# Second norm's weight on ScalarE in the stored rows, and the last four down-projection units two by two

## Chip, cores and metric

The kernel runs on one core of one Trainium2 chip. The metric is the device time of one execution in microseconds; before the change it is 1226.35 us, the median of three runs (1225.46 to 1226.62). Lower is better.

## The reference

One layer of a hybrid encoder for 1024 prompt tokens and 64 sample tokens that share the weights (1088 columns in all; the model width is 1024).

```
hn   = rmsnorm(h, pre_mix_g);   proj = hn @ w_in            # first norm
mix  = concat(SSD heads(proj), pooling groups(proj)) @ w_out
h    = h + rmsnorm(mix, post_mix_g)                          # h1
hn   = rmsnorm(h, pre_ffn_g)                                 # second norm: x * rstd(x) * weight
f    = (silu(hn @ w_gate) * (hn @ w_up)) @ w_down            # FFN
h    = h + rmsnorm(f, post_ffn_g)                            # h2
gate = sigmoid(h @ w_ple_gate)
y    = h + rmsnorm((p @ w_ple_proj) * gate, ple_norm_g)
```

Here rmsnorm(x, g) is x / sqrt(mean(x*x) + eps) * g over the model width. All of it is in float32.

## The kernel before, in words

Activations lie transposed: model width on the 128 partitions (8 blocks), tokens on the free axis, in four chunks of 272 columns. A float32 product is made of float32r halves (high part by a ScalarE cast, low part by a VectorE subtraction in the helper `sub`, L416), so each block takes three matmuls of 272 columns.

After the mixer, `out_tile` makes the w_out product of a chunk, ScalarE moves it out of PSUM with the weight of the post-mix norm (L1518), and `post_mix` goes on by pairs of blocks (four pairs, tiles of 128x544): VectorE multiplies by the norm's rstd (L1422), the residual x is added (L1431 by GpSimd, or by VectorE, as the string `XM` says for each pair: G or D), the sum h1 is stored to DRAM for later, and the class `SumSq` squares it (ScalarE, L617) and sums the squares (VectorE, L624, then L635). `rstd_job` turns the sum into rstd: small matmuls (L527), nine tiny VectorE instructions (L532 to L561), four transposes that leave rstd spread over the partitions in a PSUM bank (L565). Then `norm` multiplies each of the eight blocks by weight and rstd in one VectorE instruction (L1457).

The FFN multiplies 2x2 block matrices with seven products instead of eight (Strassen's scheme). For each pair of chunks p, `hforms(p)` builds seven combinations of the normed h (`B11`, `B21`, `T1` to `T4`, `B22`): VectorE differences (L1489), ScalarE casts (L1477), low parts (L416, tile h_T or h_B). A unit of weights has seven combinations too, and `product(q, m, ...)` (L1642) is product m of pass q: A11*B11 is 1, A12*B21 is 2, S4*B22 is 3, A22*T4 is 4, S1*T1 is 5, S2*T2 is 6, S3*T3 is 7. Three PSUM areas serve a pass: Z takes products 1, 6, 7 and 4 one on top of the other, and between them a copy or an addition must have read Z; W takes product 2, X takes 5 and then 3. `ffn()` writes out the order on TensorE: product 1 of a pass, products 4 and 3 of the pass before, then 2, 6, 5, 7 of the pass, and `until(...)` holds a product back until the reader of Z (flags s1, u2, u3) or X (x1) has been issued. Gate and up units come first (`passes`), then the down-projection (`passes2`), whose results `accum` adds into the tiles F on VectorE (L1905, first time by a ScalarE copy, L1902).

The last two down-projection units, d1_9 and d2_9, have two blocks only and are cut by chunk pair: four short passes, d1_9 and d2_9 for the first two chunks (p=0), then both for the last two (p=1). A product there is six matmuls, and the next units follow at once. When all of F of a chunk is final (`f_ready`), its squares are summed (L617, L624, L635), rstd is made, and `post_ffn` multiplies (L2089), adds h1 (L2095 GpSimd, L2098 VectorE) and splits h2 into high (L2103) and low parts (L416, tile h). The gate product of the last stage (`run_k` L509 by blocks as they are ready, `run` L492) needs h2 of chunk 0 right after the last FFN product; its weights w_pg are split on ScalarE (L463) and VectorE (L416) meanwhile.

The order of every engine's instructions is fixed beforehand by a planner (`Layout`): each step is a generator that yields requests such as `("A", 0.48, at)`, engine, planned cost and what to wait for; A is ScalarE, D VectorE, E VectorE with both operands in SBUF, G GpSimd (the planner lets no E and G overlap), S the DMA queue on SyncE, P TensorE. The planner picks the earliest start, then the lower priority number. A DMA counts as landed (`at`) 2 us plus columns divided by a rate (680 a microsecond in this stage) after its issue. On the chip each engine runs its list in order and waits at an instruction until the data are there.

At the start, `x_square` sums the squares of the first chunk of x; the string `XE` names for each chunk who squares and who adds (L772): A is ScalarE, G GpSimd, D VectorE.

Of the kernel before, what the change touches and what calls it, by code (L numbers as in the profile page):

```python
# [10 lines left out]
AF = mybir.ActivationFunctionType  # L11
ALU = mybir.AluOpType
PSUM = bass.MemoryType.PSUM

P = 128
# [16 lines left out]
SEQ_IN = '4567pppp'  # L32
NZ = 3

XM, XF, XP = 'GGGG', 'GDGD', 'GDDD'
XE = ('AG', 'AD', 'AD', 'AD')

XL = 'GPGD'
NWARM, LW = 5, 256
# [16 lines left out]
P_DT = 3  # L56
P_DTE = 1
P_DTC = 4

FAST_M, FAST_H = (3,), (3,)  # L60

# [6 lines left out]
NK = 8  # L68
# [147 lines left out]
class Layout:  # L216
# [20 lines left out]
    def spawn(self, gen, prio=5):  # L237
        self.seq += 1
        job = {"gen": gen, "prio": (prio, self.seq), "t": max(self.now, self.done), "eng": "P", "req": None, "ready": 0.0}
        if self.step(job):  # L240
            self.jobs.append(job)
            self.jobs.sort(key=lambda j: j["prio"])
# [72 lines left out]
    def until(self, cond, what=""):  # L315
        n = 0
        while not cond():
            if self.fill and not self.filling and self.fill[0][0]():
                self.filler()
                continue  # L320
            self.tick()
            n += 1
            assert n < 500, what
# [12 lines left out]
def trunk(ctx, tc, xT, par, wmix, wdt, poolw, wout, wff, wdn, wpg, wpp, pT, ssm0,  # L336
          yT, ssm_o, conv_o, pool_o, h1_d, pool_d, e_d, af_d, ac_d):
    nc = tc.nc
    ve, ac, gp, pe, sy = nc.vector, nc.scalar, nc.gpsimd, nc.tensor, nc.sync
# [16 lines left out]
    lay = Layout()  # L356
    spawn, tick, until = lay.spawn, lay.tick, lay.until
# [113 lines left out]
    def getw(name):  # L471
        until(lambda: name in W, "weights")
        return W[name][0]
# [7 lines left out]
    def mmt(n):  # L481

        return (1.0625 * n + 12) / 2400
# [270 lines left out]
    def x_square(c, k, rv, at, used):  # L754
        L = CH[c][1]
        sq_e, add_e = XE[ORD_X.index(c)]
        if not k:
# [69 lines left out]
    for i in [1, 2, 3] + MID + [12, 13, 14, 15]:  # L827
        r, at, free = early_raw.get(i, (None, None, None))
# [218 lines left out]

    spawn(dt_chain(), P_DTC)
    w = getw("in4")
# [221 lines left out]
    for t in MID:  # L1271
        w = getw(f"in{t}")
        gi = t - 8
        for c in ORD_X:
            if gi >= 0:
                L = CH[c][1]
# [90 lines left out]
    for c in ORD_Z:  # L1367
        L = CH[c][1]
# [28 lines left out]
    normed = set()  # L1397
# [7 lines left out]
    def post_mix(c, mf, ss):  # L1405

        L = CH[c][1]
        flag = []
        used = [0]
        added = [0, 0]  # L1410
        ss2 = SumSq(f"h{c}", 4, lambda: spawn(second(), 0), P_SQH)

        def two(i):
            if XM[i] != "A":
                yield n2.ok
                xr = n2.take(f"xr{c}_{i}")
                yield ("S", 0, 0)
                at = dma(xr, xT[c][:, 2 * i:2 * i + 2], 2 * L)
            yield lambda: bool(flag)
            v = mf[i // 2][:, i % 2 * 2:i % 2 * 2 + 2, :]  # L1420
            yield ("D", 0.72, 0)
            ve.tensor_tensor(v, v, flag[0][:, :L].unsqueeze(1).broadcast_to([P, 2, L]), ALU.mult)  # L1422
            used[0] += 1
            if used[0] == 4:
                banks.give(flag[0])
            if XM[i] == "A":
                yield ("S", 0, 0)
                yield ("S", 0, dma_add(v, xT[c][:, 2 * i:2 * i + 2], 2 * L))
            elif XM[i] == "G":
                yield ("G", 1.35, at)  # L1430
                gp.tensor_tensor(v, v, xr, ALU.add)  # L1431
            else:
                yield ("E", 0.73, at)
                ve.tensor_tensor(v, v, xr, ALU.add)
            if XM[i] != "A":
                n2.give(xr)
            added[i // 2] += 1
            if added[i // 2] == 2:
                dma(h1_d[c][:, i // 2 * 4:i // 2 * 4 + 4], mf[i // 2], 4 * L)
            ss2.add(v)  # L1440

        for i in range(4):
            spawn(two(i), 0)
        yield from rstd_job(ss.halves(), L, 1024.0, f"m{c}", flag, fast=c in FAST_M, free=ss.free)

        def second():
            got = []
            yield from rstd_job(ss2.halves(), L, 1024.0, f"h{c}", got, fast=c in FAST_H, free=ss2.free)
            r2 = got[0]
            left = [NK, 4, 4]  # L1450
            for m in range(NK):
                spawn(norm(m, r2, left), 0)

        def norm(m, r2, left):
            v = mf[m // 4][:, m % 4, :]
            yield ("D", 0.49, 0)
            ve.scalar_tensor_tensor(v, v, pcol("pre_ffn_g", m), r2[:, :L], ALU.mult, ALU.mult)  # L1457
            left[0] -= 1
            left[1 + m // 4] -= 1
            if not left[1 + m // 4]:  # L1460
                normed.add((c, m // 4))
            if not left[0]:
                banks.give(r2)

# [168 lines left out]
    def product(q, m, d, start):  # L1633
        u = q.u
        wf, bf = MW[m]
        until(lambda: wf in u.wf, f"{u.name} {wf}")
        until(lambda: all(u.ready(bf, p) for p in q.ps), f"{u.name} {bf}")
        w = u.wf[wf]
        for k in range(u.ks):
            for wi, xi in PASSES:  # L1640
                for p in q.ps:
                    pe.matmul(d[:, p - q.ps[0], :], w.v(wi, k), u.b(bf, xi, p, k), start=start and not k and not wi and not xi,  # L1642
                              stop=k == u.ks - 1 and wi == 1, skip_group_check=True)
            tick(3 * q.n * mmt(CW))
        if q.last:
            u.wf.pop(wf).give()
        for p in q.ps:
            u.used(bf, p)
        q.on(q, m)
# [202 lines left out]
    passes = []  # L1852
# [27 lines left out]
    ph2, ph3 = [1e9], [1e9]  # L1880
# [40 lines left out]
    units2, passes2 = [], []  # L1921
# [35 lines left out]
    for c in ORD_F:  # L1957
        L = CH[c][1]
# [56 lines left out]
    spawn(a_stream(), 1)  # L2015

    def ffn():
        prev = None
        for q in passes + passes2 + [None]:
            if q is passes[-1]:  # L2020
                ph2[0] = lay.now + 21
            if q is passes2[-5]:
                ph3[0] = lay.now
            if q is passes[0]:
                while lay.fill:
                    until(lay.fill[0][0], "fill")
                    if lay.fill:
                        lay.filler()
            if q:
                if q in passes2 and (q.i, 0) not in F:  # L2030
                    for th in range(2):
                        until(lambda: slots.free(True) >= 1, "F")
                        F[q.i, th] = slots.take(f"f{q.i}_{th}", F32, True).rearrange("p (h c t) -> p h c t", h=2, c=2)
                q.Z = bankn(q, f"z_{q.u.name}")
                product(q, 1, q.Z, True)
            if prev:
                until(lambda: "u3" in prev.f, "u3")
                product(prev, 4, prev.Z, False)
                until(lambda: "x1" in prev.f, "x1")
                product(prev, 3, prev.X, False)  # L2040
            if q:
                q.W = bankn(q, f"w_{q.u.name}")
                product(q, 2, q.W, True)
                until(lambda: "s1" in q.f, "s1")
                product(q, 6, q.Z, False)
                q.X = bankn(q, f"x_{q.u.name}")
                product(q, 5, q.X, True)
                until(lambda: "u2" in q.f, "u2")
                product(q, 7, q.Z, False)
            if q is passes[-1]:  # L2050
                n2.stay = False
                n2.drop()
            if q is passes2[-1]:
                banks.pairs = False
            prev = q


    def fv(c, m):
# [113 lines left out]
    for m in range(NK):  # L2172
        spawn(wjob(f"pg_{m}", wpg[m], "pg", 9, start=lambda: lay.now >= ph3[0],
                   keep=lambda: 0 if H2[ORD_E[0]] else 4), 3)
    ffn()

    def e_load(c, i):
# [8 lines left out]
    for c in ORD_E:  # L2186
        t0, L = CH[c]
# [6 lines left out]
        for i in range(4):  # L2194
# [4 lines left out]
            def scale(q, i=i, e=e):  # L2199
                yield ("A", 0.5)  # L2200
                ac.activation(e[:, q], e[:, q], AF.Identity, scale=pcol("ple_norm_g", 2 * i + q))
# [170 lines left out]
```

## Time and profile before

| | |
|---|---|
| median of 3 runs | 1226.35 us |
| the profiled execution: its own time / its span | 1227.99 / 1226.2 us |
| TensorE busy | 1201.8 us (98%) |
| VectorE, ScalarE, GpSimd busy | 862.6, 577.0, 65.2 us |
| mean granted TensorE clock | 0.991 |

The span is from the first to the last instruction of the profiled execution; 1.8 us of its own time lie around it. TensorE is the engine that sets the time: it is busy nearly throughout, so only the few stretches in which it waits, or in which its clock is granted at half, can give time back. A busy share of another engine matters only in such a stretch.

### The profile page before, as it was taken

The page shows a single profiled execution, that of the slowest core. Times are in us where ns is not written, and L with a number is a line of the kernel's source. Part 1 is how long each engine was busy: PE and PEld are TensorE (multiplying, and loading weights), DVE is VectorE, ACT ScalarE, POOL GpSimd, SP SyncE. Part 2 cuts the span into 40 slices and gives each one's busy share as a digit, 9 for nine tenths or more (in the row PEclk, how much of TensorE's full clock was granted, in tenths as well). Part 3 has the DMA queues.
Part 4 walks back from the last instruction along what each step waited for, and adds up shares of the span by engine and source line. Part 5 has one row for each costly group of instructions (what it writes and reads, how often), then busy time and mean ns, then how long its engine had stood idle before and what let it go on. Part 6 is the DMA issues. An engine that isn't in the chain of part 4 may idle for free.

```text
span 1226.2 us, 23743 instructions
## 1 busy us (share of the span) xinstructions
PE 1201.8 (98%) x9641; PEld 1181.8 (96%) x9641; DVE 862.6 (70%) x1572; ACT 577.0 (47%) x1123; POOL 65.2 (5%) x56
## 2 busy tenths in 40 slices
PE   8999999999999899999999999999999999999997
PEld 6999999999999899999999999999999999988996
DVE  5796867775798786776667667766746556688765
ACT  6354657964457444443444444443432212346543
POOL 2000000111241000000000000000000000002011
PEclk8999999999999899999999999999999999999998
DMA  6122122143446044444344334337978676334422
GB/s 226 42 74 80 62 96 92 52 133 114 135 161 225 14 137 148 153 153 133 134 162 145 130 138 163 132 122 263 404 280 291 213 254 231 115 96 132 142 74 83
DMA packets 73201, 182.01 MB, mean 148 GB/s; under 512 B 8636, under 2 KB 16644, under 8 KB 73092
## 3 DMA queue, kind: packets, MB, share of 16 engines
q1 hardware_dynamic: 73092, 180.50, 42.7%
q8 instruction: 75, 1.23, 0.4%
q14 instruction: 34, 0.28, 0.1%
HBM read 121.75 MB, written 58.72 MB: 147 GB/s over the span
## 4 chain that ended last, share of the span: by engine, by line
PE 92%; DVE 3%; ACT 2%; DMA 1%; issue 1%; SPq 0%; DVEq 0%; ACTq 0%
PE psall L1642 55%; PE psall L492 29%; PE psall L509 2%; PE psall L527 1%; PE psall L1128 1%; PE psall L565 1%; PE psall L1157 1%; PE psall L1122 1%; DVE f L1905 0%; DMA raw_in<-in_wmix_dram 0%; PE psall L1243 0%; PE psall L736 0%; DMA raw_out<-in_wout_dram 0%; DVE w_out L416 0%; DMA raw_pg<-in_wpg_dram 0%
## 5 line engine op out<-in xcount | busy, mean ns | idle before, releaser
L492 PE MATMUL psall<-x,w_in 128*128 128x272 f32 x1440 | 193.7, 291 | 0.0
L492 PEld LDWEIGHTS psall<-x,w_in 128*128 128x128 f32 x1440 | 184.0, 188 | 3.3 <-issue 2.8
L1905 DVE TENSOR_TENSOR f<-f,psall 128x544 f32<-128x544 f32 (+1 forms) x96 | 60.4, 636 | 68.8 <-PE psall L1642 67.0
L1642 PE MATMUL psall<-h_T,w_g_S 128*128 128x272 f32 x792 | 104.4, 292 | 3.2 <-DVE h_T L416 2.9
L1642 PEld LDWEIGHTS psall<-h_T,w_g_S 128*128 128x128 f32 x792 | 102.5, 193 | 3.6 <-DVE h_T L416 3.1
L1642 PE MATMUL psall<-al_T,w_d_S 128*128 128x272 f32 x768 | 100.4, 289 | 1.4 <-DVE f L1905 0.9
L1642 PE MATMUL psall<-h_T,w_u_S 128*128 128x272 f32 x792 | 100.8, 287 | 0.0
L1642 PEld LDWEIGHTS psall<-al_T,w_d_S 128*128 128x128 f32 x768 | 97.7, 188 | 2.3 <-ACT w_pg L463 0.9
L1642 PEld LDWEIGHTS psall<-h_T,w_u_S 128*128 128x128 f32 x792 | 99.6, 188 | 0.0
L492 PE MATMUL psall<-mix,w_out 128*128 128x272 f32 x720 | 93.5, 289 | 0.0
L492 PEld LDWEIGHTS psall<-mix,w_out 128*128 128x128 f32 x720 | 90.9, 188 | 0.0
L1642 PE MATMUL psall<-al_B,w_d_A 128*128 128x272 f32 x528 | 72.3, 289 | 2.7 <-DVE w_d_A L416 2.6
L492 PE MATMUL psall<-h,w_pg 128*128 128x272 f32 x576 | 74.7, 289 | 0.0
L492 PEld LDWEIGHTS psall<-h,w_pg 128*128 128x128 f32 x576 | 72.8, 188 | 0.0
L1642 PEld LDWEIGHTS psall<-al_B,w_d_A 128*128 128x128 f32 x528 | 68.5, 188 | 3.3 <-DVE w_d_A L416 3.1
L1642 PE MATMUL psall<-h_B,w_g_A 128*128 128x272 f32 x528 | 69.9, 288 | 0.0
L1642 PE MATMUL psall<-h_B,w_u_A 128*128 128x272 f32 x528 | 69.8, 288 | 0.0
L1642 PEld LDWEIGHTS psall<-h_B,w_u_A 128*128 128x128 f32 x528 | 67.7, 188 | 0.0
L1642 PEld LDWEIGHTS psall<-h_B,w_g_A 128*128 128x128 f32 x528 | 67.6, 188 | 0.0
L1570 ACT CAST w_d_A<-raw_d 128x512 fp32r<-128x512 f32 (+3 forms) x44 | 22.3, 522 | 70.2 <-PE psall L1642 35.1
L1570 ACT CAST w_d_S<-raw_d 128x512 fp32r<-128x512 f32 (+3 forms) x54 | 26.5, 532 | 56.4 <-DVE raw_d L1594 33.8
L416 DVE TENSOR_TENSOR w_u_S<-raw_u,w_u_S 128x512 fp32r<-128x512 f32 x44 | 30.3, 688 | 26.5 <-ACT w_u_S L1570 26.4
(407 smaller groups left out, 2211.7 us busy)
## 6 DMA issues: line engine op xcount, KB each, us to landing
af_dram<-a_T SPq DMA_DIRECT2D x88, 272.0 KB, 2.2
al_T<-af_dram SPq DMA_DIRECT2D x44, 544.0 KB, 6.1
af_dram<-a_B SPq DMA_DIRECT2D x66, 272.0 KB, 2.7
al_B<-af_dram SPq DMA_DIRECT2D x33, 544.0 KB, 6.4
raw_g<-in_wff_dram SPq DMA_DIRECT2D x22, 512.0 KB, 3.8
raw_u<-in_wff_dram SPq DMA_DIRECT2D x22, 512.0 KB, 3.7
raw_in<-in_wmix_dram SPq DMA_DIRECT2D x15, 512.0 KB, 3.8
raw_d<-in_wdn_dram SPq DMA_DIRECT2D x14, 512.0 KB, 4.6
```

The costliest lines, as they stand in the source:

```text
L416: eng.tensor_tensor(lo, src, hi.bitcast(F32), ALU.subtract)
L492: pe.matmul(out, lhsT, rhs, start=i == 0, stop=i == n - 1)
L509: pe.matmul(out, w.v(wi, k), act.v(xi, k, L), start=first and n == 0, stop=not left and n == 2)
L527: pe.matmul(ps[:n, 500 + 4 * i + j:501 + 4 * i + j], acc[:, n * j:n * j + n], ones[:, 0:1], start=True, stop=True)
L565: pe.transpose(pss[i][:, n * j:n * j + n], y[:, 4 * i + j:4 * i + j + 1].broadcast_to([n, P]), ident[:n, :n])
L1122: pe.matmul(py[:L, 256 * g:256 * g + 256], ct[:, g, t0:t0 + L], state[:, 256 * g:256 * g + 256], start=True, stop=True)
L1128: pe.matmul(pst[:, 256 * g:256 * g + 256], bk[:L, 128 * g:128 * g + 128], xw[:L, 4 * g:4 * g + 4].rearrange("p h q -> p (h q)"), start=Tru ...
L1157: pe.matmul(pyt[64 * r:64 * r + 64, P * b:P * b + L], xdt[:L, h], es[h // 4][:L, h % 4, :L], start=first, stop=True, skip_group_check=True)
L1570: ac.copy(v[:, 0], src)
L1642: pe.matmul(d[:, p - q.ps[0], :], w.v(wi, k), u.b(bf, xi, p, k), start=start and not k and not wi and not xi, stop=k == u.ks - 1 and wi == ...
L1905: ve.tensor_tensor(v[:, sl], v[:, sl], src[:, pl], ALU.add)
```

## The change

There are three parts. First, in `post_mix` the weight of the second norm leaves `norm`: h1 of each pair is stored as soon as it is added (four stores of 272 KB per chunk instead of two of 544 KB), and when ScalarE has squared a pair and the store has landed, ScalarE multiplies the two blocks by the weight in place. `norm` is then one VectorE multiplication by rstd per half (128x1088) instead of four instructions of 128x272. Second, the residual of the fourth pair of each chunk is added by VectorE instead of GpSimd, and the sums of squares of the first chunk of x too. Third, `ffn()` works on groups of passes: one pass a group as before, but the last four down-projection passes are two groups of two whose products alternate.

```diff
-XM, XF, XP = 'GGGG', 'GDGD', 'GDDD'
-XE = ('AG', 'AD', 'AD', 'AD')
+XM, XF, XP = 'GGGD', 'GDGD', 'GDDD'
+XE = ('AD', 'AD', 'AD', 'AD')
...
+P_SCL = 0
...
-            added[i // 2] += 1
-            if added[i // 2] == 2:
-                dma(h1_d[c][:, i // 2 * 4:i // 2 * 4 + 4], mf[i // 2], 4 * L)
-            ss2.add(v)
+            at = dma(h1_d[c][:, 2 * i:2 * i + 2], v, 2 * L)
+            ss2.add(v, lambda: spawn(scale(i, v, at), P_SCL))
+
+        def scale(i, v, at):
+
+            for q in range(2):
+                yield ("A", 0.48, at)
+                ac.activation(v[:, q], v[:, q], AF.Identity, scale=pcol("pre_ffn_g", 2 * i + q))
+            scaled[i // 2] += 1
...
-        def norm(m, r2, left):
-            v = mf[m // 4][:, m % 4, :]
-            yield ("D", 0.49, 0)
-            ve.scalar_tensor_tensor(v, v, pcol("pre_ffn_g", m), r2[:, :L], ALU.mult, ALU.mult)
...
+        def norm(h, r2, left):
+            yield lambda: scaled[h] == 2
+            yield ("D", 1.27, 0)
+            ve.tensor_tensor(mf[h], mf[h], r2[:, :L].unsqueeze(1).broadcast_to([P, 4, L]), ALU.mult)
...
-        prev = None
-        for q in passes + passes2 + [None]:
+        groups = [[q] for q in passes + passes2[:-4]] + [passes2[-4:-2], passes2[-2:], []]
+        prev = []
+        for qs in groups:
+            for q in qs:
...
                 q.Z = bankn(q, f"z_{q.u.name}")
                 product(q, 1, q.Z, True)
-            if prev:
-                until(lambda: "u3" in prev.f, "u3")
-                product(prev, 4, prev.Z, False)
-                until(lambda: "x1" in prev.f, "x1")
-                product(prev, 3, prev.X, False)
-            if q:
+            for q in prev:
+                until(lambda: "u3" in q.f, "u3")
+                product(q, 4, q.Z, False)
+            for q in prev:
+                until(lambda: "x1" in q.f, "x1")
+                product(q, 3, q.X, False)
+            for q in qs:
                 q.W = bankn(q, f"w_{q.u.name}")
                 product(q, 2, q.W, True)
+            for q in qs:
                 until(lambda: "s1" in q.f, "s1")
                 product(q, 6, q.Z, False)
+            for q in qs:
                 q.X = bankn(q, f"x_{q.u.name}")
                 product(q, 5, q.X, True)
+            for q in qs:
                 until(lambda: "u2" in q.f, "u2")
                 product(q, 7, q.Z, False)
```

## Rows read from the trace of the kernel before

**Rows 1.** Busy time by stretch: length, each engine's busy us (instructions), TensorE clock, DMA share, GB/s
```profile
500.00:600.00 100.00, 100.00 (x801) 100.00 (x801) 67.07 (x101) 44.26 (x75) 0.00 (x0) 1.00 0.44 151
...
385.00:395.00 10.00, 10.00 (x85) 10.00 (x84) 8.54 (x20) 6.65 (x14) 5.34 (x4) 1.00 0.51 184
405.00:415.00 10.00, 6.49 (x48) 5.84 (x46) 9.35 (x15) 4.74 (x9) 0.00 (x0) 1.00 0.00 0
417.00:420.00 3.00, 3.00 (x15) 3.00 (x14) 2.39 (x2) 0.66 (x2) 0.00 (x0) 0.50 0.00 0
1084.00:1109.60 25.60, 22.70 (x172) 21.02 (x171) 20.41 (x50) 12.77 (x23) 1.36 (x1) 1.00 0.24 70
1109.60:1118.00 8.40, 6.96 (x57) 6.54 (x57) 8.37 (x12) 5.95 (x10) 1.36 (x1) 1.00 0.45 129
```
**Rows 2.** TensorE in order of time around the last chunk's norm: start, us, [idle before]
```profile
409.54 1.79 PE L1642 MATMUL psall<-h_B,w_g_S 128*128 128x272 f32 x12 [1.74 <-DVE xr L1685]
...
413.20 0.39 PE L1642 MATMUL psall<-h_T,w_g_S 128*128 128x272 f32 x1 [0.37 <-ACT h_T L1477]
416.44 7.29 PE L1642 MATMUL psall<-h_T,w_g_S 128*128 128x272 f32 x35 [2.85 <-DVE h_T L416]
```
**Rows 3.** VectorE in order of time, the same stretch
```profile
404.46 1.72 DVE L1457 SCALAR_TENSOR_TENSOR mixf<-mixf,cp,psall 128x272 f32<-128x272 f32 x4 [1.23 <-PE psall L565]
406.22 1.29 DVE L1489 TENSOR_TENSOR mixf<-mixf,mixf 128x1088 f32<-128x1088 f32 x1
407.43 1.72 DVE L1457 SCALAR_TENSOR_TENSOR mixf<-mixf,cp,psall 128x272 f32<-128x272 f32 x4
409.06 0.43 DVE L1685 TENSOR_TENSOR xr<-xr,psall 128x272 f32<-128x272 f32 x1
...
415.11 1.28 DVE L416 TENSOR_TENSOR h_T<-mixf,h_T 128x1088 fp32r<-128x1088 f32 x1
```
**Rows 4.** All engines in order of time, the last chunk's residual and squares
```profile
388.26 2.61 DVE L1422 TENSOR_TENSOR mixf<-mixf,psall 128x544 f32<-128x544 f32 x4 [1.32 <-PE psall L565]
...
391.75 2.71 POOL L1431 TENSOR_TENSOR mixf<-mixf,xr 128x544 f32<-128x544 f32 x2
...
395.66 0.67 ACT L617 ACTIVATE xr<-mixf 128x544 f32<-128x544 f32 x1
...
396.99 0.72 DVE L624 TENSOR_TENSOR p<-p,xr 128x544 f32<-128x544 f32 x1
```
**Rows 5.** Prices by line: duration in ns, shortest/median/longest
```profile
L2081 ACT ACTIVATE f<-f,cp x32: 506/508/518, 1097.5 to 1161.6; 128x272 f32<-128x272 f32 x32
```
**Rows 6.** SyncE's DMA issues from 305 to 400 us
```profile
DMA to landing us min/median/max: 1.7/2.7/4.7
```
**Rows 7.** TensorE in order of time, the last four FFN passes and the gate product
```profile
1083.47 0.92 PE L1642 MATMUL psall<-al_B,w_d_A 128*128 128x272 f32 x6
...
1095.27 0.92 PE L1642 MATMUL psall<-al_B,w_d_S 128*128 128x272 f32 x6
...
1099.12 0.60 PE L527 MATMUL psall<-cp,sq_f 128*68 128x1 f32 x8
...
1101.87 0.65 PE L1642 MATMUL psall<-al_T,w_d_A 128*128 128x272 f32 x3 [0.90 <-DVE f L1905]
1102.35 0.40 PE L565 MATMUL psall<-cp,t_f 68*128 68x68 f32 x4
...
1109.66 3.17 PE L509 MATMUL psall<-h,w_pg 128*128 128x272 f32 x24
...
1114.66 2.39 PE L509 MATMUL psall<-h,w_pg 128*128 128x272 f32 x17 [0.78 <-DVE h L416]
```
**Rows 8.** The additions of the squares of x by engine: shortest/median/longest ns
```profile
L772 DVE TENSOR_TENSOR acc_x<-acc_x,sqx x21: 429/431/441, 22.9 to 54.6; 128x272 f32<-128x272 f32 x21
L772 POOL TENSOR_TENSOR acc_x<-acc_x,sqx x7: 764/765/1705, 10.3 to 16.8; 128x272 f32<-128x272 f32 x7
```
**Rows 9.** VectorE's waits from 8 to 33 us: us in total, times, longest
```profile
DVE t_x L532 <- PE psall L527: 3.4, 1, 3.4
```

More of the change, by code (lines that the diff above doesn't have):

```diff
@@ L1409, in post_mix @@
         used = [0]
-        added = [0, 0]
+        scaled = [0, 0]
         ss2 = SumSq(f"h{c}", 4, lambda: spawn(second(), 0), P_SQH)
@@ L1449, in second @@
             r2 = got[0]
-            left = [NK, 4, 4]
-            for m in range(NK):
-                spawn(norm(m, r2, left), 0)
-        def norm(m, r2, left):
-            v = mf[m // 4][:, m % 4, :]
-            yield ("D", 0.49, 0)
-            ve.scalar_tensor_tensor(v, v, pcol("pre_ffn_g", m), r2[:, :L], ALU.mult, ALU.mult)
+            left = [2]
+            for h in range(2):
+                spawn(norm(h, r2, left), 0)
+        def norm(h, r2, left):
+            yield lambda: scaled[h] == 2
+            yield ("D", 1.27, 0)
+            ve.tensor_tensor(mf[h], mf[h], r2[:, :L].unsqueeze(1).broadcast_to([P, 4, L]), ALU.mult)
             left[0] -= 1
-            left[1 + m // 4] -= 1
-            if not left[1 + m // 4]:
-                normed.add((c, m // 4))
+            normed.add((c, h))
             if not left[0]:
@@ L2017, in ffn @@
     def ffn():
-        prev = None
-        for q in passes + passes2 + [None]:
[L2020 to L2028, printed above, removed]
-            if q:
+        groups = [[q] for q in passes + passes2[:-4]] + [passes2[-4:-2], passes2[-2:], []]
+        prev = []
+        for qs in groups:
+            for q in qs:
+                if q is passes[-1]:
+                    ph2[0] = lay.now + 21
+                if q is passes2[-5]:
+                    ph3[0] = lay.now
+                if q is passes[0]:
+                    while lay.fill:
+                        until(lay.fill[0][0], "fill")
+                        if lay.fill:
+                            lay.filler()
                 if q in passes2 and (q.i, 0) not in F:
@@ L2035, in ffn @@
                 product(q, 1, q.Z, True)
-            if prev:
-                until(lambda: "u3" in prev.f, "u3")
-                product(prev, 4, prev.Z, False)
-                until(lambda: "x1" in prev.f, "x1")
-                product(prev, 3, prev.X, False)
-            if q:
+            for q in prev:
[5 more added lines that the diff above has]
+            for q in qs:
                 q.W = bankn(q, f"w_{q.u.name}")
                 product(q, 2, q.W, True)
+            for q in qs:
                 until(lambda: "s1" in q.f, "s1")
                 product(q, 6, q.Z, False)
+            for q in qs:
                 q.X = bankn(q, f"x_{q.u.name}")
                 product(q, 5, q.X, True)
+            for q in qs:
                 until(lambda: "u2" in q.f, "u2")
                 product(q, 7, q.Z, False)
-            if q is passes[-1]:
+            if qs and qs[-1] is passes[-1]:
                 n2.stay = False
                 n2.drop()
-            if q is passes2[-1]:
+            if qs and qs[-1] is passes2[-1]:
                 banks.pairs = False
-            prev = q
+            prev = qs
     def fv(c, m):
```

## Prediction

> **What bounds the kernel now.** I read the shares of busy time first, then busy time by stretch, then TensorE's waits and, around each of them, the engines in order of time. TensorE is the bound: in the middle of the FFN it is busy for 100.00 of 100 us with 801 matmuls, so a full-size matmul costs 0.125 us and no other engine's work matters there [rows 1]. Two places that the change touches break this pattern.
>
> The first is the start of the FFN. From 405 to 415 us TensorE is busy for 6.49 us of 10 while VectorE is busy for 9.35 [rows 1]. TensorE waits there three times, 1.74 + 0.37 + 2.85 = 4.96 us, always for something that stands behind the last chunk's norm in VectorE's list [rows 2]: the first wait ends with an addition (L1685) that comes right after the second four norm instructions, the last one with the low part of T2 (L416), which needs both halves normed [rows 3]. After these waits the granted clock is 0.50, the lower of its two levels [rows 1]; 35 matmuls take 7.29 us there instead of 35 x 0.125 = 4.37, which is 2.92 us more [rows 2].
>
> The second is the run of four short down-projection passes. From the start of product 2 of the first (1083.47) to the gate product (1109.66) are 26.19 us [rows 7]. In it lie 27 products of six matmuls, 27 x 6 x 0.125 = 20.2 us, and the two small groups of a rstd, at most 0.60 + 0.40 = 1.0 us. So 5.0 us are stalls (the view by stretch shows 25.60 - 22.70 = 2.9 of them as idle [rows 1]; the rest is hidden in the modelled ends of matmuls). They come because a product here is only 0.75 us long, and the VectorE addition that must free Z or X before the next one is not done in that time: the row with 0.90 us of waiting for L1905 is one of them [rows 7]. Behind the passes the gate product stands still too, waiting for h2 of chunk 0 [rows 7].
>
> **The change part by part.** *Norm.* Per half, four instructions go (1.76 us from the first's start to the next instruction in the first half, 1.63 in the second) and one of 128x1088 comes. With both operands in SBUF such a one takes 1.21 from start to start [rows 3]; with one operand in PSUM, as here, two of half the size take 2 x 2.61 / 4 = 1.30 [rows 4]. Both halves lie on the path, so the gain is 1.76 + 1.63 - 2 x 1.30 = 0.8 us, between 0.7 and 1.0. The other three chunks' norms lie under a TensorE that does not wait; they count for nothing.
>
> *Weight on ScalarE.* Eight instructions of 0.508 us come in each chunk (the same form, ScalarE with a column of weights [rows 5]): 16.3 us in all, 4.06 in the last chunk. Three chunks are hidden by the w_out products and the p products under which ScalarE has room; in the last one ScalarE has 3.35 us free of 10 in the stretch where the squares are taken [rows 1], and the scales have until rstd arrives at 404.46 [rows 3], 7.5 us after the last sum's addition at 396.99 [rows 4]. I count 0. Without that cover they would stand ahead of the last square and cost up to 4.06. Each scale waits for its store: median landing 2.7 us, longest 4.7 [rows 6], and the planner allows 2 + 544 / 680 = 2.8. Behind a scale that waits stand squares, casts of h_B and copies out of PSUM; TensorE would wait for these copies in the end. The eight more stores are issues on SyncE, which then holds back only later stores and loads; I count 0 for them too.
>
> *Residual of the fourth pair.* The last two GpSimd additions take 2.71 us [rows 4], so GpSimd ends 1.35 us sooner; VectorE pays one more addition of this size, 0.72 [rows 4]. The last square waits for the last addition and for its turn on ScalarE. The bounds are 1.35 gained and 0.72 lost; since the GpSimd chain ends the row of squares, I take 1.35 - 0.72 = 0.6 us gained.
>
> *First chunk's sums.* Seven additions move: 7 x 0.431 = 3.0 us on VectorE instead of 0.765 to 1.7 each on GpSimd [rows 8]. VectorE stands 3.4 us waiting for the rstd matmul right behind them [rows 9], which covers them, and that matmul is placed by a fixed planned time. I count 0; if the additions landed ahead of the low parts that TensorE needs, up to 3.0 would be lost.
>
> *Passes two by two.* Between products 6 and 7 of a pass now stand three products (2.25 us) instead of one (0.75), so the addition in between has three times as long. If all stalls went, 5.0 us would be gained. But h2 of chunk 0 has to come sooner as well. Its last input is product 4 of the second pass. Count the short products in both orders (1 | 2, 6, 5, 7 | 1 | 4, 3 | 2, 6, 5, 7 | 1 | 4 against 1, 1 | 2, 2, 6, 6, 5, 5, 7, 7 | 1, 1 | 4, 4): it is the fourteenth in both, and fourteen follow. So it comes sooner only by the stalls ahead of it. Thirteen products take 1095.27 - 1083.47 = 11.80 us instead of 9.75 [rows 7]: 2.05 us. Against that, the squares and sums of its last two pairs now come one right behind the other, which costs one more addition, 0.7 us. From there to the last part of h2 the chain is 1114.66 - 1095.27 = 19.4 us long [rows 7]. If its length stays, 2.05 - 0.7 = 1.35 us are gained, and TensorE waits for h2 instead of for Z and X. If it shrinks with the stalls in VectorE's list, up to 5.0. VectorE is busy for 20.41 + 8.37 = 28.78 of these 34 us [rows 1], 85%, so there is room, but little. I take 2.5, nearer to the lower bound because of that share.
>
> The sum is 0.8 + 0.6 + 2.5 = 3.9 us. Against the profiled execution's own 1227.99 us it gives 1224.1; that execution stands 1.64 above the median of the runs, so for a median I forecast 1226.35 - 3.9 = 1222.5 us.
>
> **Rivals.** *The clock holds too.* With 1.4 us less waiting at the FFN's start, 3.6 of the 4.96 us remain. If the granted clock then stays at 1.00, the 2.92 us come back as well: 1222.5 - 2.9 = 1219.5 us. For it: the waits that are left are split by two runs of matmuls. Against it: the longest wait, 2.85 us, shrinks only by what VectorE's list in front of T2 gets shorter. The Trainium skill, "TensorE: Matmul & The Clock Gate", section "HAM oscillation", says that idle gaps put TensorE's clock back to half; the trace agrees, 0.50 right after the waits, and by that rule a short enough rest of them gives this case.
>
> *The gains are given back.* VectorE, at 85% in the tail and 9.35 of 10 us at the FFN's start, has the same work to do in less time; stalls move from Z and X to h2, and the scales take away what GpSimd's shorter chain gave. Then the tail brings its lower bound, 1.35, and the start nothing: 1225.0 us. For it speak the wait of the gate product that is there already and the unchanged place of product 4; against it, that VectorE's idle time in the tail is itself mostly waiting for the short products.
>
> *Slower: ScalarE sets the last chunk's path.* Place: the last chunk's scales, if they are planned ahead of its last square. Price: 4.06 us for all eight, and 4.7 - 2.8 = 1.9 us for each store that lands as late as the slowest. Against the remaining gains of 0.8 + 2.5 it decides from 3.3 us on, and is measurable at 5.8: all eight and one late store, 5.96, give 1226.35 + 5.96 - 3.3 = 1229.0 us. For it: ScalarE works in order and a scale's planned landing time is close to the median, so half of the stores land later. Against it: 3.35 us of 10 are free, and the store of a pair is issued before its square. The Trainium skill, "ScalarE: Activation LUTs", section "Rules for kernel authors", speaks against this part of the change: multiplications are for VectorE, not ScalarE. For these shapes the rows say otherwise, 0.508 us on ScalarE against 1.72 / 4 = 0.43 on a VectorE that is the fuller of the two [rows 3, 5]; by the rule the last chunk would lose 4.06 - 0.8 = 3.3 us, by the rows it gains 0.8.
>
> **Chances.** Forecast, with 2.5 to 6 us gained: 0.45. Clock holds too: 0.17. Given back, within 2.4 us of before: 0.26. ScalarE's path: 0.12. A difference of 0.2% (2.45 us) is about what a measurement of this kernel can tell from none, so faster is 0.45 + 0.17 = 0.62, the same 0.26, slower 0.12. The range reaches down to all gains at their upper bounds, 1.0 + 1.35 + 2.92 + 5.0 = 10.3 us, less a little (1216.5), and up past the case of gains given back (1227.5); most of the slower case lies outside.
>
> **What would show it.** Right: one instruction of 1.2 to 1.3 us in place of each four at L1457; TensorE's waits between 405 and 417 us down from 4.96 to about 3.6; 35 matmuls after them still at 0.50; the short passes down from 26.2 us to some 22, with a longer wait for h2 behind them. Wrong: ScalarE waiting for a store to h_dram in front of the last chunk's squares; the last square no earlier than 395.66; waits for L1905 as many as before; a granted clock of 0.50 in a stretch that had 1.00; or a changed order in the lists of the middle of the kernel that makes TensorE wait where it did not.

## The result, and the profile after

The changed kernel takes 1219.05 us (median of 5 runs, 1216.35 to 1221.81), the kernel before 1226.62 beside it: ratio 0.993, 95% interval 0.9908 to 0.9952. The forecast was faster by 3.9 us, to 1222.5; the gain is 7.6 us, inside the range, but above the 2.5 to 6 us that the forecast counted as its own case. The time is nearest to that of the rival "the clock holds too", 1219.5.

The profiled execution has a span of 1217.3 us, 8.9 less than before. Line numbers after are those before plus one up to L1409, and plus 4 to 10 behind it: the norm is L1463, the FFN's product L1646. The FFN's start, TensorE in order of time after (to be read against [rows 2]):

```profile
385.16 0.40 PE L566 MATMUL psall<-cp,t_m 68*128 68x68 f32 x4
385.37 10.13 PE L493 MATMUL psall<-p,w_pp 128*128 128x272 f32 x78
395.33 2.43 PE L1646 MATMUL psall<-h_B,w_g_A 128*128 128x272 f32 x18
...
408.25 1.77 PE L1646 MATMUL psall<-h_B,w_g_S 128*128 128x272 f32 x12 [1.36 <-DVE p L1689]
...
411.86 4.74 PE L1646 MATMUL psall<-h_T,w_g_S 128*128 128x272 f32 x35 [0.20 <-DVE h_T L417]
416.44 3.18 PE L1646 MATMUL psall<-h_B,w_u_A 128*128 128x272 f32 x24
```

The three waits, 4.96 us, have become two of 1.36 + 0.20 = 1.56, and the 35 products behind them take 4.74 us where they took 7.29. The stretches after say why (columns as in [rows 1]):

```profile
405.00:415.00 10.00, 8.43 (x65) 7.95 (x64) 9.90 (x13) 5.18 (x9) 0.00 (x0) 1.00 0.00 0
417.00:420.00 3.00, 3.00 (x26) 3.00 (x26) 2.80 (x5) 0.80 (x3) 0.00 (x0) 1.00 0.00 0
```

The granted clock is 1.00 from 417 to 420 us, where it was 0.50, and 26 matmuls fit where 15 did. The norm on VectorE after, against [rows 3]:

```profile
400.90 1.29 DVE L1463 TENSOR_TENSOR mixf<-mixf,psall 128x1088 f32<-128x1088 f32 x1 [0.43 <-PE psall L566]
402.23 1.29 DVE L1493 TENSOR_TENSOR mixf<-mixf,mixf 128x1088 f32<-128x1088 f32 x1
403.44 1.28 DVE L1463 TENSOR_TENSOR mixf<-mixf,psall 128x1088 f32<-128x1088 f32 x1
```

It is shorter, from 4.69 us (404.46 to 409.15) to 3.82, as the sum had it; and it starts 3.56 us sooner, which the sum did not have. The tail after, in order of time ([rows 7]):

```profile
1092.16 1.03 PE L1646 MATMUL psall<-al_T,w_d_S 128*128 128x272 f32 x6 [0.54 <-DVE f L1909]
...
1098.87 0.39 PE L510 MATMUL psall<-h,w_pg 128*128 128x272 f32 x1 [1.57 <-ACT h L2113]
1099.69 7.69 PE L510 MATMUL psall<-h,w_pg 128*128 128x272 f32 x47 [0.43 <-DVE h L417]
...
1107.68 5.15 PE L493 MATMUL psall<-h,w_pg 128*128 128x272 f32 x39
...
1135.09 0.65 PE L528 MATMUL psall<-cp,sq_e 128*68 128x1 f32 x8 [0.78 <-DVE sq_e L636]
```

```profile
1098.80:1108.00 9.20, 8.70 (x58) 8.50 (x59) 9.01 (x12) 5.50 (x11) 1.72 (x1) 0.81 0.69 216
```

Among the short passes one wait is left, 0.54 us, where TensorE before stands for 0.74, 0.41, 0.19, 0.90 and 0.53. Behind them it stands 1.57 us for h2, and the 47 products that follow run in part at the lower clock (0.81 on the mean of that stretch). To read gains without the accidents of the start (below), I cut each profile at the same four places: the start of the first FFN product, of the product that comes behind the 35 that follow the norm's waits, of the first gate product, and of the kernel's last group of matmuls (us; the first column from the span's start, the others the time between neighbours, worked out from the rows of each trace):

```
                first FFN   to end of   to first   to last
                product     the 35      gate       product
before          396.27      27.30       686.09     109.71
after           395.33      21.11       682.43     111.59
only_weight     399.76      19.33       686.15     109.63
only_residual   396.20      24.61       686.13     109.90
only_start      393.59      24.69       685.89     109.94
only_pairs      394.89      28.85       683.36     111.43
clock_kept      394.82      26.03       686.27     109.71
tail_kept       398.66      21.11       682.55     111.49
no_residual     398.35      19.32       682.67     111.68
no_pairs        395.01      21.10       685.90     109.81
norm_eight      395.68      22.36       683.74     111.45
no_scale        396.20      20.56       682.57     111.42
start_kept      393.38      21.10       682.39     111.63
h2_first        393.14      21.10       688.67     108.53
```

From before to after: 0.94 + 6.19 + 3.66 - 1.88 = 8.9 us. The 3.66 us are not the pairs' alone. The last 262 matmuls ahead of the gate product, where the pairs are, go from 37.55 to 34.82 us, 2.73 less. Some 1.4 us come from a wait of 1.19 us at 882.82 us before, for the low part of a weight (w_d_A): it is in the five traces whose norm has its weight on VectorE (before, only_residual, only_start, only_pairs, clock_kept) and in none of the other nine. And the first 3500 matmuls behind the FFN's start take 438.25 us after and 437.68 before, 0.57 more, with no wait in either; no run tells why.

### The profile page after: what moved, and what is told of

The parts are those of the page before. It is cut to its first block, busy times and chain, and to the rows that moved or that the text cites. A ratio compares the mean times of both kernels' runs of the same rounds, so it can differ in the third digit from the quotient of the medians.

```text
span 1217.3 us, 23775 instructions
## 1 busy us (share of the span) xinstructions
PE 1198.8 (98%) x9641; PEld 1180.8 (97%) x9641; DVE 866.0 (71%) x1559; ACT 587.4 (48%) x1155; POOL 53.2 (4%) x45
## 4 chain that ended last, share of the span: by engine, by line
PE 91%; DVE 4%; DMA 2%; ACT 2%; issue 1%; SPq 0%; DVEq 0%; ACTq 0%
PE psall L1646 55%; PE psall L493 28%; PE psall L510 2%; PE psall L528 1%; DMA al_B<-af_dram 1%; PE psall L1129 1%; PE psall L1158 1%; PE psall L566 1%; PE psall L1123 1%; DMA raw_d<-in_wdn_dram 1%; PE psall L737 0%; PE psall L1244 0%; DVE f L2108 0%; DMA raw_in<-in_wmix_dram 0%; DVE h L417 0%
## 5 line engine op out<-in xcount | busy, mean ns | idle before, releaser
L1646 PE MATMUL psall<-h_T,w_g_S 128*128 128x272 f32 x792 | 101.7, 288 | 0.2 <-DVE h_T L417 0.2
L1646 PE MATMUL psall<-h_T,w_u_S 128*128 128x272 f32 x792 | 100.8, 287 | 0.0
L1646 PEld LDWEIGHTS psall<-h_T,w_g_S 128*128 128x128 f32 x792 | 100.0, 188 | 0.5 <-DVE h_T L417 0.4
L1646 PE MATMUL psall<-al_T,w_d_S 128*128 128x272 f32 x768 | 99.5, 288 | 0.5 <-DVE f L1909 0.5
L1646 PEld LDWEIGHTS psall<-h_T,w_u_S 128*128 128x128 f32 x792 | 99.7, 188 | 0.0
L1646 PEld LDWEIGHTS psall<-al_T,w_d_S 128*128 128x128 f32 x768 | 97.5, 188 | 0.9 <-DVE f L1909 0.8
L1646 PE MATMUL psall<-al_B,w_d_A 128*128 128x272 f32 x528 | 71.1, 288 | 1.5 <-DVE w_d_A L417 1.5
L1646 PE MATMUL psall<-h_B,w_g_A 128*128 128x272 f32 x528 | 70.2, 288 | 0.0
L1646 PE MATMUL psall<-h_B,w_u_A 128*128 128x272 f32 x528 | 69.8, 288 | 0.0
L1646 PEld LDWEIGHTS psall<-al_B,w_d_A 128*128 128x128 f32 x528 | 68.0, 188 | 1.7 <-DVE w_d_A L417 1.7
L1646 PEld LDWEIGHTS psall<-h_B,w_g_A 128*128 128x128 f32 x528 | 67.8, 188 | 0.0
L1646 PEld LDWEIGHTS psall<-h_B,w_u_A 128*128 128x128 f32 x528 | 67.7, 188 | 0.0
```

## The experiments

**The parts alone.** Each edit puts one part of the change into the kernel before; the four ran on one chip, beside 1227.28 us for the kernel before.

```diff
only_residual:
-XM, XF, XP = 'GGGG', 'GDGD', 'GDDD'
+XM, XF, XP = 'GGGD', 'GDGD', 'GDDD'
only_start:
-XE = ('AG', 'AD', 'AD', 'AD')
+XE = ('AD', 'AD', 'AD', 'AD')
only_pairs: the new ffn(); only_weight: the new scale(), norm() and stores of h1
```

> The kernel before with the second norm's weight on ScalarE and the two norm multiplications per chunk alone (residuals, first chunk's sums and order of passes as before). Theory of the prediction, norm term: 0.8 us less waiting at the FFN's start (4.96 to about 4.2 us), the clock falls there as before, so 0.8 us gained. Rival, clock: the shorter list is enough to keep the clock at 1.00 behind the waits, 0.8 + 2.9 = 3.7 us gained. Rival, ScalarE: the scales delay the last square, no gain or up to 3.3 us lost.

> The kernel before with the fourth pair's residual on VectorE alone. Theory of the prediction: the last sum ends 0.6 us sooner, 0.6 us gained, the clock falls as before. Rival: the sum of squares hangs on GpSimd's additions alone, up to 1.35 us gained. Rival: the addition on VectorE delays the last chunk's list, 0 to 0.7 us lost.

> The kernel before with the first chunk's sums of squares on VectorE alone. Theory of the prediction: 0. Rival, from the trace after, where the first FFN product starts 0.94 us sooner than before: GpSimd's additions hold VectorE's first low parts up, and 0.9 us are gained at the start and kept to the end.

> The kernel before with the last four passes two by two alone. Theory of the prediction: 2.5 us gained, bounds 1.35 and 5.0; the short passes shrink from 26.2 to about 22 us and the gate product waits longer for h2. Rival, from the trace after, where the clock is granted at 0.81 on the mean behind the wait for h2: the gathered wait lets the clock fall, which takes 1.8 us back, so 0.7 us gained. Rival: gains come from the other parts only, 0.

| run | median us (range) | ratio, 95% interval |
|---|---|---|
| only_weight | 1223.45 (1222.26 to 1224.6) | 0.9965, 0.9953 to 0.9978 |
| only_residual | 1225.02 (1223.57 to 1225.92) | 0.9981, 0.9972 to 0.999 |
| only_start | 1225.32 (1222.73 to 1227.47) | 0.9983, 0.9972 to 0.9993 |
| only_pairs | 1226.43 (1222.82 to 1227.13) | 0.9983, 0.9972 to 0.9994 |

Every part gains. Together they would make 0.88%, the change makes 0.70%, with an interval of 0.48 to 0.92, so this sum alone does not show whether the parts add up. The eleven executions of only_pairs fall apart: three of 1222.8 to 1223.4 us with a mean granted clock of 0.995, eight of 1225.4 to 1227.1 with 0.990 to 0.994. Its profiled execution is one of the eight; the clock fell twice at its FFN's start, which takes 28.85 us.

The weight alone empties the FFN's start of waits (19.33 us), but pays for it ahead of the FFN. TensorE in only_weight:

```profile
393.06 2.51 PE L493 MATMUL psall<-p,w_pp 128*128 128x272 f32 x18 [1.00 <-DVE mixf L1463]
395.84 4.08 PE L493 MATMUL psall<-p,w_pp 128*128 128x272 f32 x30 [0.27 <-ACT e L1829]
399.76 1.29 PE L1646 MATMUL psall<-h_B,w_g_A 128*128 128x272 f32 x9
```

The first FFN product comes at 399.76, 3.5 us later than before; with one more wait of 1.49 us at 375.00, also for e, 2.76 of the 3.5 us stand in the rows as waits. The same trade is there in no_residual, and gone in after and no_pairs: with the fourth residual on VectorE the products of p wait 0.3 us.

In only_start and in the kernel before, the waits at the FFN's start are the same to 0.02 us. TensorE in only_start:

```profile
406.87 1.78 PE L1642 MATMUL psall<-h_B,w_g_S 128*128 128x272 f32 x12 [1.74 <-DVE xr L1685]
...
410.53 0.39 PE L1642 MATMUL psall<-h_T,w_g_S 128*128 128x272 f32 x1 [0.38 <-ACT h_T L1477]
413.76 4.67 PE L1642 MATMUL psall<-h_T,w_g_S 128*128 128x272 f32 x35 [2.84 <-DVE h_T L416]
```

Behind the same three waits 35 products take 4.67 us here and 7.29 in [rows 2]. The granted clock over them is 1.00 here. So the fall of the clock is not fixed by the waits alone. The Trainium skill, "TensorE: Matmul & The Clock Gate", section "Part 1: The HAM clock gate", says that the monitor of the clock runs freely, so that one program meets it differently from run to run; these two traces, of kernels that differ only at the start, fit that.

**The clock at the FFN's start.** clock_kept is the kernel before with work of no use in the wait:

```diff
+                if q is passes[1]:
+                    keep_busy(26)
                 product(q, 6, q.Z, False)
...
+    def keep_busy(n):
+        b = banks.order[0]
+        hi = HF[0]["B11"][0][0]
+        for _ in range(n):
+            pe.matmul(psall[:, b, :CW], hi[:, 0, :P], hi[:, 1, :CW], start=True, stop=True)
```

> Before, with 26 products of no use (their result is overwritten) put on TensorE ahead of the last product that waits at the start of the FFN: they run while TensorE would stand for the 2.85 us wait, and nothing else is changed. Theory (part of the gain is TensorE's clock, which fell to half in the 35 products behind that wait and cost 2.9 us there): the wait is gone from the rows, the granted clock is 1.00 in the 35 products, they take 4.7 us and not 7.3, and the time falls by 2 to 3 us, to a ratio of 0.976 to 0.984 of a per cent scale read as 0.9976 to 0.9984. Rival (the clock's fall is by chance of the execution, and the gain was the shorter waits alone): ratio within 0.9992 to 1.0008.

(The ratios meant are 0.9976 to 0.9984.) Measured: 1225.0 us (1224.28 to 1227.07) beside 1227.4, ratio 0.9978 (0.9969 to 0.9988). TensorE in clock_kept:

```profile
408.11 1.92 PE L1642 MATMUL psall<-h_B,w_g_S 128*128 128x272 f32 x12 [1.75 <-DVE xr L1685]
409.83 2.92 PE L1642 MATMUL psall<-h_B,w_g_A 128*128 128x272 f32 x12
412.55 3.65 PE L2021 MATMUL psall<-h_B 128*128 128x272 f32 x26
416.03 4.98 PE L1642 MATMUL psall<-h_T,w_g_S 128*128 128x272 f32 x36
```

The products behind the long wait run at the full rate, 36 in 4.98 us. In this execution the clock fell behind the first wait instead (12 products in 2.92 us, usually 1.67), so the profile shows only part of the gain; the medians show 2.4 us (1.5 to 3.8 by the interval). Over whole executions the mean granted clock is 0.993 to 0.997 in the nine of clock_kept, and 0.991 in eight of the thirteen of the kernel before beside it. The clock there is worth that much by itself: counted from the FFN's start, the products behind the long wait begin no sooner than in the kernel before (21.21 us against 20.17).

**The tail's clock.** tail_kept is after with 16 products of no use ahead of the first gate product.

```diff
+                if c == ORD_E[0]:
+                    kb = getw("pg_0").t[0]
+                    for _ in range(16):
+                        pe.matmul(d[:, 0][:, :2 * P], kb[:, 0, :], kb[:, 0:2, :], start=True, stop=True)
```

> After, with 16 products of no use (256 columns, overwritten by the next) put on TensorE between the last short pass and the first gate product, where after's trace has a wait of 1.57 us for h and then 47 products that took 7.69 us at a mean granted clock near half. Theory (the gathered wait lets the clock fall and costs 1.8 us there): the 47 products take about 5.9 us, and the time is 1.5 to 2 us below after's, ratio to before about 0.9915. Rival (what TensorE gains there is given back at the next wait for the last chunk's norms, as 1.6 us were in after): ratio 0.993, as after.

1218.75 us (1218.04 to 1222.4), ratio 0.9926 (0.9911 to 0.994): no gain over the 0.993 of after can be told, whose own interval is as wide as 0.9908 to 0.9952. TensorE in tail_kept:

```profile
1102.32 0.29 PE L510 MATMUL psall<-h,w_pg 128*128 128x272 f32 x1
1102.99 3.56 PE L510 MATMUL psall<-h,w_pg 128*128 128x272 f32 x24 [0.38 <-DVE h L417]
1107.33 3.14 PE L510 MATMUL psall<-h,w_pg 128*128 128x272 f32 x23 [0.79 <-DVE h L417]
1110.31 0.60 PE L528 MATMUL psall<-cp,sq_f 128*68 128x1 f32 x8
1110.77 5.15 PE L493 MATMUL psall<-h,w_pg 128*128 128x272 f32 x39
```

With less time lost to the clock, TensorE waits 0.79 us for the next h instead: from the first gate product to the next group it takes 8.45 us here, 8.81 in after, 8.52 in before. The lower clock in after hides under h2's chain; my theory of 1.8 us lost there falls, and the rival holds. Traces without any filler there say the same: in no_residual, norm_eight and start_kept the granted clock stays at 1.00 behind that wait, TensorE then waits 0.78 or 0.79 us for the next h, and from the gate to the end they take 111.68, 111.45 and 111.63 us, against 111.59 in after. So the 1.88 us given back behind the gate are not the clock's. TensorE in no_residual:

```profile
1100.34 0.39 PE L510 MATMUL psall<-h,w_pg 128*128 128x272 f32 x1 [1.59 <-ACT h L2113]
1101.17 3.56 PE L510 MATMUL psall<-h,w_pg 128*128 128x272 f32 x24 [0.44 <-DVE h L417]
1105.52 3.17 PE L510 MATMUL psall<-h,w_pg 128*128 128x272 f32 x23 [0.78 <-DVE h L417]
```

**Leaving a part out.**

```diff
no_residual:
-XM, XF, XP = 'GGGD', 'GDGD', 'GDDD'
+XM, XF, XP = 'GGGG', 'GDGD', 'GDDD'
no_pairs: the ffn() of the kernel before
```

> After with the fourth residual back on POOL: weight by ScalarE, pairs and first chunk's sums stay. Theory (the weight in the stored rows needs the residual early, since ScalarE's scales stand behind it: only_weight paid 2.8 us of waits among the products of the first half's p for what it saved at the FFN's start): those waits of 1.0 and 1.8 us come back, the first FFN product starts 2 to 4 us later than in after, and the ratio is 0.9945 to 0.9955. Rival (the parts add up, the residual is worth its 0.0019 alone): ratio 0.9949 with no waits at the products of p.

> After with the last four units of the FFN one by one again. Theory (the pairs' gain in after is the short waits taken out, 3.7 us to the first gate product, less 1.6 us that come back at the last chunk's norms): the start of the FFN as in after, the short passes with the waits of before, first gate product 3 to 4 us later than in after, and the end 2 us later: ratio 0.9945 to 0.995. Rival (the waits of the short passes are made up later, since the gate product waits for h2 with or without them): ratio within 0.0008 of after's 0.993.

no_residual: 1219.55 us (1218.91 to 1220.61), ratio 0.9928 (0.9916 to 0.9941). no_pairs: 1220.31 (1219.95 to 1220.52), 0.9933 (0.9919 to 0.9947). Both lie within 0.0003 of the whole change, though each part gains alone; as the ratio of after is uncertain by 0.0022, a loss of some 2 us could stay unseen this way. For the residual the expected waits of 1.0 us and 1.7 us came back and the first FFN product comes 3.02 us later than in after, as expected, but then the FFN's start is 1.79 us shorter (19.32 against 21.11): the wait in part changes its place. My ratio of 0.9945 and more and the rival's 0.9949 both lie outside the interval. For the pairs the table has the two terms: 685.90 - 682.43 = 3.47 us gained up to the gate, 111.59 - 109.81 = 1.78 us given back behind it, 1.7 left.

**The norm's length.** norm_eight is after with the norm in eight instructions again, a column of ones for the weight.

```diff
...
-            ve.tensor_tensor(mf[h], mf[h], r2[:, :L].unsqueeze(1).broadcast_to([P, 4, L]), ALU.mult)
...
+            v = mf[m // 4][:, m % 4, :]
+            yield lambda: scaled[m // 4] == 2
+            yield ("D", 0.49, 0)
+            ve.scalar_tensor_tensor(v, v, ones[:, 0:1], r2[:, :L], ALU.mult, ALU.mult)
...
```

> After with the norm in eight instructions again, each the old form with a column of ones in the weight's place; ScalarE's scales stay. It gives back the shorter work of VectorE behind rstd and keeps the rest of the change. Theory (what moved the waits at the FFN's start is that rstd comes sooner, 400.9 against 404.5 us, because the rows' sums stand earlier; the shorter norm is worth the 0.7 to 1.0 us of the sum): waits at the FFN's start of 2.2 to 3.0 us in all instead of 1.6, clock at 1.00 or fallen once, ratio 0.994 to 0.996. Rival (the two long instructions are the whole gain): waits of 4 to 5 us as before, ratio 0.997 to 0.999.

1221.75 us (1220.93 to 1222.9), ratio 0.9956 (0.9942 to 0.9969). The waits behind the norm are 2.57 us (1.56 in after), and the end of the 35 comes 1.25 us later; another 1.3 us are lost up to the gate, 0.4 of it in the wait for h2. The other 0.9 are spread evenly over the first 3500 matmuls behind the FFN's start, which take 439.14 us (438.25 in after) without a wait; what makes them slower is open. The ratio and the waits that the theory named hold, but leaving out the shorter norm costs more than the 0.7 to 1.0 us that it gave for it. VectorE and TensorE in norm_eight:

```profile
386.44 0.40 PE L566 MATMUL psall<-cp,t_m 68*128 68x68 f32 x4
...
401.84 1.72 DVE L1464 SCALAR_TENSOR_TENSOR mixf<-mixf,cp,psall 128x272 f32<-128x272 f32 x4 [0.55 <-PE psall L566]
...
413.55 4.65 PE L1649 MATMUL psall<-h_T,w_g_S 128*128 128x272 f32 x35 [2.57 <-DVE h_T L417]
```

The granted clock is 1.00 behind this wait of 2.57 us too.

**ScalarE's scales.**

no_scale is after without the scales, so it leaves out the weight of the second norm, and ScalarE has no store of h1 to wait for.

```diff
-            for q in range(2):
-                yield ("A", 0.48, at)
-                ac.activation(v[:, q], v[:, q], AF.Identity, scale=pcol("pre_ffn_g", 2 * i + q))
+            yield ("S", 0, 0)
             scaled[i // 2] += 1
```

> After with ScalarE's 32 scales left out, so that the second norm has no weight. Theory (ScalarE has room for the scales, they cost nothing): waits at the FFN's start of 1.4 to 1.8 us as in after, ratio within 0.001 of 0.993. Rival (the scales stand in front of the squares and of the evacuations of the last chunk): first FFN product 0.5 to 1.5 us sooner, ratio 0.9915 to 0.9925.

1218.41 us (1218.06 to 1219.36), ratio 0.9929 (0.9916 to 0.9942). The first wait at the FFN's start is 0.82 us instead of 1.36, the first FFN product no sooner, the time that of after. The scales cost nothing that can be measured, though the Trainium skill, "ScalarE: Activation LUTs", section "Rules for kernel authors", sends multiplications to VectorE: on a ScalarE with room, 32 of them at 516 ns are free here.

**A version that may be faster.** All the traces so far show the clock at half from around 10 us, behind a wait for the first chunk's x. start_kept is after with ten products of no use in that wait:

```diff
+                if k == NK // 2:
+                    kb = jbank("kb")
+                    for _ in range(10):
+                        pe.matmul(kb[:, :L], w.v(0, 0), X[c].v(0, 0, L), start=True, stop=True)
+                    banks.give(kb)
```

> After with ten products of no use on TensorE at 8 us, where the second half of the first chunk's x is waited for (0.9 us in after, 0.6 to 1.5 us in other executions) and behind which the granted clock is 0.50 to 12 or 15 us. Theory (that wait lets the clock fall): granted clock 1.00 from 10 us on, the first weights' products done 1 to 2 us sooner, ratio 0.9915 to 0.9925. Rival (at that time the transfers, busy all the time to 18 us, set the pace): the clock is kept but new waits for weights take its place, ratio 0.993; second rival (ten products are too few or too late): clock 0.50 and a ratio of 0.993 to 0.9935.

The stretch from 10 to 16 us, in after and then in start_kept:

```profile
10.00:16.00 6.00, 6.00 (x34) 4.17 (x34) 5.48 (x13) 6.00 (x15) 0.00 (x0) 0.53 1.03 410
```

```profile
10.00:16.00 6.00, 5.86 (x50) 4.03 (x51) 5.25 (x13) 6.00 (x14) 0.00 (x0) 1.00 1.03 410
```

The clock is 1.00, 50 matmuls run instead of 34, and the first FFN product comes at 393.38 instead of 395.33. 1217.37 us (1217.02 to 1218.04), ratio 0.9921 (0.9906 to 0.9936): all five runs lie below the five of no_scale on the same chip, which are as fast as after, by 1.0 us in the medians. After itself did not run beside it, and the intervals overlap.

h2_first adds to start_kept a higher priority for the first chunk's post_ffn:

```diff
-            sumf[c] = SumSq(f"f{c}", 4, lambda: spawn(post_ffn(c, sumf[c], 2 + n if n else 1), 3 if n else 0), P_SQ + n if n else 0)
+            sumf[c] = SumSq(f"f{c}", 4, lambda: spawn(post_ffn(c, sumf[c], 2 + n if n else -1), 3 if n else -1), P_SQ + n if n else 0)
```

> start_kept with one number more changed: the norm of the first chunk's h2 stands ahead of the last short passes' additions in VectorE's order (in after its first multiplication starts at 1095.39, 1.6 us after VectorE has the sum's result, behind two additions that wait for TensorE). Theory (with the pairs, the wait of 1.57 us for h2 and the 0.8 to 1.8 us given back behind it are this chain, which is late in VectorE's order): the gate's products wait under 0.5 us for their first h, those behind it wait less, ratio 0.9895 to 0.991, that is 1.5 to 3 us below start_kept. Rival (the additions moved back then hold TensorE's banks): a new wait of 0.5 to 2 us for an addition among the short passes, ratio 0.992 as start_kept or above.

1221.12 us (1219.95 to 1222.31), ratio 0.9955 (0.9941 to 0.9968). TensorE in h2_first:

```profile
1098.47 3.09 PE L1651 MATMUL psall<-al_T,w_d_A 128*128 128x272 f32 x12 [6.47 <-DVE f L1914]
1101.36 1.72 PE L1651 MATMUL psall<-al_B,w_d_S 128*128 128x272 f32 x12
1102.91 3.17 PE L510 MATMUL psall<-h,w_pg 128*128 128x272 f32 x24
```

The gate waits for nothing any more, and from it to the end are 108.53 us instead of 111.63; but the additions that were moved back free a bank 6.47 us late, the granted clock is 0.50 behind that wait, and the way to the gate is 688.67 us instead of 682.39. It is the rival, at three times its price: h2 cannot be had sooner in this way.

## Why the prediction was right in sign and short in size

- **Norm, 0.8 us.** Right for the last chunk: 4.69 to 3.82 us is 0.87. The step "the other three chunks' norms ... count for nothing" failed: they stand in VectorE's list ahead of the last chunk's chain. That chain begins with the post-mix rstd product (t_m). In the kernel before TensorE has it here:

```profile
387.83 0.40 PE L565 MATMUL psall<-cp,t_m 68*128 68x68 f32 x4
...
388.27 8.16 PE L492 MATMUL psall<-p,w_pp 128*128 128x272 f32 x63
```

  63 products of p follow it before the FFN, after the change 78: it comes 10.17 us ahead of the first FFN product instead of 8.44, 1.73 us sooner. norm_eight loses 0.93 of that, and the last chunk's own norm stands behind t_m, so it is the other three chunks' norms that make this difference.
- **Residual, 0.6 us (bounds -0.72 to 1.35).** Mis-sized: alone it takes the norm's start from 8.19 us behind the first FFN product to 6.69, 1.50 sooner, and the waits from 4.96 to 3.37. It too starts the chain sooner (9.39 us ahead against 8.44), which my bounds, taken from the last square on, left out. All parts together reach 5.57. So the waits fell by 3.40 us, not 1.4; the norm's start (2.62 sooner) and length (0.87 shorter) add up to that. The norm's start in only_residual:

```profile
402.89 1.72 DVE L1457 SCALAR_TENSOR_TENSOR mixf<-mixf,cp,psall 128x272 f32<-128x272 f32 x4
```

- **Scales on ScalarE, 0.** Right by no_scale; and in after the last square is at 392.79 us, not later than 395.66, so the rival "ScalarE sets the last chunk's path" is out:

```profile
392.79 0.65 ACT L618 ACTIVATE xr<-mixf 128x544 f32<-128x544 f32 x1
```

- **First chunk's sums, 0 (up to 3.0 lost).** Too low: only_start is 2.0 us faster (0.9 to 3.4 by the interval). What the rows show of it is a wait of 0.32 us for the low part of x at 29.78, which is in the five traces without this part and in none with it. The rest is not located: the first FFN product comes 2.68 us sooner in only_start, but 1.4 us sooner in only_pairs and clock_kept too, whose start is that of before, so the 0.94 us of after lie within what the start varies by itself. The wait in the kernel before:

```profile
29.78 0.52 PE L509 MATMUL psall<-x,w_in 128*128 128x272 f32 x2 [0.32 <-DVE x L749]
```

- **The clock.** The forecast left it at 0.50 and gave 2.9 us to a rival; 2.55 came back in the profile, 2.4 by clock_kept. What I held against that rival, that the wait of 2.85 us would shrink only a little, is the term mis-sized above: it is 0.20 now.
- **Pairs, 2.5 us (1.35 to 5.0).** Right in mechanism, too high in size: as the prediction said, TensorE waits for h2 instead of for Z and X. Alone they gain 2.73 us up to the gate and give 1.72 back behind it, 1.0 left, under the lower bound; left out of the whole they are worth 1.7. What the sum did not have is the part given back behind the gate. It is not the clock's (above); in after 0.29 us of it lie in the first group of gate products, and 1.1 are waits that the trace before has not (0.17, 0.78 and 0.17 us at 1130.41, 1135.09 and 1159.65); the rest stands in no row. "The gains are given back" is true of this part by half.

The sum against the profile: 0.94 up to the FFN, 3.40 of waits, 2.55 of clock and 0.24 of small gaps at its start, 1.78 behind it: 8.9 us. That the time met the clock rival's 1219.5 within half a microsecond is partly luck: the rival's 1.4 us of waits were 3.40, and the pairs' 2.5 us were 1.0 to 1.7.

## What to carry to other kernels

An instruction made shorter on an engine that is full can count for all work listed behind it, also under a TensorE that does not wait: follow the late chain back to its first entry in that engine's list before calling the cover free. A wait on TensorE behind which its clock falls costs more than its length (2.55 us more at the FFN's start). Products of no use in the gap measure that price: 2.4 us there, nothing in the tail, where the work behind waits for h2 anyway. Where the wait itself cannot be taken out, they may be left in, as in start_kept. Parts that feed the same wait need not add up: without the residual the FFN's start got shorter while the way to it got longer, so leave each part out of the whole before keeping it.

## What had not been expected

Waits equal to 0.02 us, three of 4.96 us in all, were followed by the lower clock in one execution (35 products in 7.29 us) and not in another (4.67). The wait for h2 ahead of the gate was followed by it in after (1.57 us), and not in start_kept (1.59) or norm_eight (1.97). So a single profile over- or understates what a part is worth; the five executions of after run from 1216.35 us, with a mean granted clock of 0.997, to 1221.81, with 0.992. The rise at the start differs in the same way: over 10 to 16 us the mean granted clock was 0.50 in before and 0.77 in only_start. Two waits ahead of the FFN, for t_g (L562), came to 0.7 us together in start_kept and to 2.4 us in tail_kept, whose code is the same there; no run tells why.
